# Products of 512, 256 and 384 columns over token parts side by side, exponentials and row steps kept away from the ends of gate sums, and spaced copies of rpb

## The chip, the cores and the metric

The kernel runs on one core of one Trainium2 chip. The metric is the time of one execution on the device, in microseconds; several runs are taken and their median counts. Besides the timed runs there is one profiled execution, and every row of the trace in this document is from such an execution. The engines are named as in the profile: PE is the matrix engine, PEld its loading of weights, DVE the vector engine, ACT the scalar engine, POOL GpSimd, SP the engine that issues most transfers. A "product" is one matrix multiplication instruction of PE.

## The reference

One layer of a hybrid diffusion backbone, in float32, for 128 context tokens and 256 latent tokens (384 tokens in all), with 2048 channels:

```python
sh1, sc1, g1, sh2, sc2, g2 = modulation(cond, w_mod_l, b_mod_l)
h = rms_norm(x, n1) * (1 + sc1) + sh1
q, k, v, u = project_in(h, w_in_l, qg_l, kg_l)
attn = attend(q, k, v)
# token_mixing
na = attn.reshape(b, t, D_NA) @ w_na_proj
fn = fourier_mix(u) @ w_fnet_proj
g_na, g_fn = jnp.split(jax.nn.sigmoid(h @ w_gate), 2, axis=-1)
x = x + g1 * ((g_na * na + g_fn * fn) @ w_o)
h2 = rms_norm(x, n2) * (1 + sc2) + sh2
# swiglu
a, g = jnp.split(h2 @ w_gate_up, 2, axis=-1)
x = x + g2 * ((jax.nn.silu(g) * a) @ w_down)
```

The attention of the latent tokens adds a position bias, which is gathered from the small table `rpb`.

## The kernel before

**Products in three parts.** Each operand x of a large product is kept as a high part H (x rounded to the type F32R) and a low part L = x - H. `mm3` (L146) issues three products: aH·bH, aH·bL and aL·bH. The first operand of a product is held in PE as weights, the second streams through it column by column. In the gate and the feed-forward up stages the weights are blocks of 128x128 of the weight matrix (wH, wL) and the streamed operand is h, 384 token columns wide (hH and hL, separate tiles for each of the 16 channel blocks).

**Weights.** All weight matrices come through one list of units of 256 rows by 512 columns. `next_unit` (L208) splits the unit that will be needed two units later: ACT casts it to wh (L143), DVE subtracts to get wl (L144). It then lets the next transfer be issued on SP, and returns the oldest split unit. The instructions of each engine stand in the order in which the program writes them.

**Side work.** Generators that are paced by `Paced.tick` write a step of side work between units: `rows` (the modulation rows, 16 transfers of w_mod and 32 steps on DVE, L329, for each half of a row), the Fourier branch and the attention. In the gate stage `front` holds the branch and `rows`; it is ticked three times in each unit, twice in `next_unit` and once before the third of the four sums (`mid_unit`). `Paced.tick` adds the rate to what is due, returns if less than `least` is due, and else steps until less than one is due.

**Attention.** `attention_pair` (L846) works through the ticks of `PAIR` (L44); in a tick with `e0` or `e1` ACT makes exponentials with their sums (L932), DVE takes the reciprocal (L940) and ACT scales (L942).

**Gate sums.** Eight chunks of 512 gate columns (L1018), each with eight units and four sums `po[f]` in the four `mm` banks of PSUM, which the next chunk takes again. Behind the last unit each sum is copied to SBUF (`gst`, L1032; the first two by DVE while exponentials are recent, the others by ACT) and stored to `s_gate` in DRAM by four transfers issued by ACT (L1035). In the stage behind it `load_gates` (L1053) fetches them, ACT takes the sigmoid (L1084), and DVE multiplies the projections by it (L1092).

**Feed-forward.** Six parts; in each, for four blocks f of the hidden width, first the gate half (`half` = 1, ACT's SiLU, L1319), then the other (DVE multiplies, L1321). Sums come from a ring of seven banks (`acc_tile`). The first four blocks go through another path (`late_norm`), as the norm isn't ready yet. In the last part each product is split at once for w_down (L1323).

**rpb.** `expand_rpb` (L247) makes seven copies of 512 KB from DRAM to DRAM, which give the bias as a diagonal view. It is one of the generators in `behind` in the last input group (L656), stepped once in each unit.

Of the kernel before, what the change touches and what calls it, by code (L numbers as in the profile page):

```python
# [19 lines left out]
P = 128  # L20
# [12 lines left out]
CH = 512  # L33
# [68 lines left out]
def trunk_kernel(ctx: ExitStack, tc: tile.TileContext, io: dict):  # L102
# [47 lines left out]

    def warm_sqrt():

        warm = small.tile([P, 1], F32, tag="warm", bufs=1, name=nm("warm"))
        nc.scalar.activation(out=warm, in_=ones[:, 0:1], func=AF.Sqrt)
# [73 lines left out]

    hH = [None] * KT
    hL = [None] * KT  # L230

    def new_h(kt):
        hH[kt] = hpool.tile([P, TOK], F32R, tag=f"tH{kt}", name=nm(f"hH{kt}_"))
        hL[kt] = hpool.tile([P, TOK], F32R, tag=f"tL{kt}", name=nm(f"hL{kt}_"))
        return hH[kt], hL[kt]

    s_qkvu = [dram.tile([P, NT, CH], F32, tag=f"sq{i}", name=f"s_qkvu{i}") for i in range(8)]
    s_gate = [dram.tile([P, 4, TOK], F32, tag=f"sg{i}", name=f"s_gate{i}") for i in range(8)]
# [27 lines left out]
    with ExitStack() as ph:  # L266
# [170 lines left out]
        with ExitStack() as pha:  # L437
# [377 lines left out]
        qks, vs, biases = [], [], []  # L815
        soft = deque(maxlen=3)
# [29 lines left out]
        def attention_pair(hp, wk, values_before):  # L846
# [171 lines left out]
        for fc8 in range(8):  # L1018
            po = [mm_tile() for _ in range(4)]
            sts = []  # L1020
            for u in range(0, KT, 2):
                wH, wL = next_unit()
                for f in range(4):
                    s = slice(f * P, (f + 1) * P)
                    if f == 2:
                        mid_unit()
                    for kk in range(2):
                        k = u + kk
                        mm3(po[f][:, :TOK], wH[:, kk, s], wL[:, kk, s], hH[k], hL[k], k == 0, k == KT - 1)
                    if u == KT - 2:  # L1030
                        st = gst.tile([P, TOK], F32, tag="st", name=nm("gst"))
                        (nc.vector.tensor_copy if f < 2 and any(soft) else nc.scalar.copy)(st, po[f][:, :TOK])  # L1032
                        sts.append(st)
            for f, st in enumerate(sts):
                nc.scalar.dma_start(s_gate[fc8][:, f], st)  # L1035
        br_work.drain()
        front.clear()
# [230 lines left out]

    def silus(sg, bs):
# [20 lines left out]
    for part, nf in enumerate(FF_PARTS):  # L1290
# [5 lines left out]
        for c4 in range(nf // 4):  # L1296
            for half in (1, 0):
                po = [acc_tile() for _ in range(4)]
                bs = []
                for u in range(0, KT, 2):  # L1300
                    wH, wL = next_unit()
                    for f in range(4):
                        s = slice(f * P, (f + 1) * P)
                        for kk in range(2):
                            k = u + kk
                            xH, xL = wide(k) if facc is None else (hH[k], hL[k])
                            mm3(
                                po[f][:, : xH.shape[1]], wH[:, kk, s], wL[:, kk, s], xH, xL, k == 0, k == KT - 1
                            )
# [8 lines left out]
                        elif half:  # L1318
                            nc.scalar.activation(out=sg[:, f], in_=po[f][:, :TOK], func=AF.Silu)  # L1319
                        else:  # L1320
                            nc.vector.tensor_mul(sg[:, f], sg[:, f], po[f][:, :TOK])  # L1321
                            if nf == 4:
                                work.step()  # L1323
# [84 lines left out]
```

## Time and profile before

| what | value |
|---|---|
| median of 3 runs | 2050.86 us (2049.79 to 2052.56) |
| the profiled execution | 2052.19 us |
| its span (first to last instruction) | 2050.4 us |
| mean granted clock of PE | 0.998 of full |
| PE, DVE, ACT busy | 2025.8, 1248.0, 757.9 us |
| bytes moved | 390.46 MB, mean 190 GB/s |

Rows of the trace that follow have a start in us from the beginning of the span, a duration in us, the engine, the line of kernel.py, the operation, what is written from what (`out<-in`), the shape and a count; in brackets stands how long the engine was idle before it, and what ended that wait. Matmuls overlap: the distance from start to start tells the rate of PE, not the duration of one.

### The profile page before, as it was taken

What the parts mean: (1) busy time and instruction counts of PE and PEld (TensorE: products, weight loads), DVE (VectorE), ACT (ScalarE), POOL (GpSimd) and SP (SyncE); (2) the same over time, 40 slices, a digit from 0 to 9 for tenths busy, and PEclk for the clock granted to TensorE, in tenths of its full rate; (3) what the DMA queues carried; (4) which work ended last, traced back from release to release, by engine and by line L of the source; (5) the groups of instructions that cost most, each with busy time, mean ns of one, the idle gap of its engine ahead of it and who ended that gap; (6) DMA issues with size and microseconds to landing.
All of it is one profiled execution on the core that took longest, in us unless ns stands there. A gap on an engine that the chain in (4) does not pass through costs nothing.

```text
span 2050.4 us, 27528 instructions
## 1 busy us (share of the span) xinstructions
PE 2025.8 (99%) x10986; PEld 1843.8 (90%) x10986; DVE 1248.0 (61%) x1528; ACT 757.9 (37%) x1135; POOL 43.1 (2%) x92
## 2 busy tenths in 40 slices
PE   7999999999999999999999999999999999999999
PEld 4668788999999999889998999899989998999897
DVE  4746889788987777765854444545454334333456
ACT  4433232456665434334523332222222232223222
POOL 1000000000001000010000000000000000000000
PEclk9999999999999999999999999999999999999999
DMA  9996979677776776754455555455554444444453
GB/s 332 328 338 222 309 232 315 215 217 212 228 212 181 258 248 194 250 168 154 124 167 156 152 163 155 144 153 155 155 163 134 124 129 127 129 128 123 136 163 123
DMA packets 220384, 390.46 MB, mean 190 GB/s; under 512 B 28464, under 2 KB 77632, under 8 KB 220256
## 3 DMA queue, kind: packets, MB, share of 16 engines
q1 hardware_dynamic: 213088, 382.13, 59.5%
q10 hardware_dynamic: 4672, 6.31, 0.9%
q8 instruction: 86, 1.41, 0.3%
q0 software_dynamic: 2496, 0.27, 0.1%
q14 instruction: 42, 0.34, 0.1%
HBM read 371.81 MB, written 20.51 MB: 191 GB/s over the span
## 4 chain that ended last, share of the span: by engine, by line
PE 94%; DMA 3%; DVE 2%; ACT 1%; issue 0%; SPq 0%; ACTq 0%; DVEq 0%
PE mm L147 19%; PE mm L149 19%; PE mm L148 19%; PE at L147 11%; PE at L149 11%; PE at L148 11%; PE at L404 1%; DMA wm<-in_w_mod 1%; DMA wraw<-in_w_in 1%; PE at L893 1%; PE at L979 1%; PE at L958 1%; DMA wmr<-in_w_mod 1%; DVE accr L329 0%; DMA xc<-in_x_prompt 0%
## 5 line engine op out<-in xcount | busy, mean ns | idle before, releaser
L144 DVE TENSOR_TENSOR wl<-wraw,wh 128x1024 fp32r<-128x1024 f32 (+1 forms) x464 | 559.1, 1205 | 668.5 <-ACT wh L143 667.3
L143 ACT CAST wh<-wraw 128x1024 fp32r<-128x1024 f32 (+1 forms) x464 | 480.9, 1038 | 1032.0 <-PE at L148 272.9
L147 PE MATMUL mm<-hH,wh 128*128 128x384 f32 x1152 | 389.4, 338 | 2.4 <-DVE gst L1032 2.4
L149 PE MATMUL mm<-hH,wl 128*128 128x384 f32 x1152 | 385.5, 335 | 0.0
L148 PE MATMUL mm<-hL,wh 128*128 128x384 f32 x1152 | 385.2, 334 | 0.0
L329 DVE SCALAR_TENSOR_TENSOR accr<-wmr,csz,accr 128x1024 f32<-128x1024 f32 x240 | 304.8, 1278 | 5.2 <-DMA wmr<-in_w_mod 5.1
L147 PEld LDWEIGHTS mm<-hH,wh 128*128 128x128 f32 x1152 | 216.3, 188 | 8.1 <-issue 4.3
L148 PEld LDWEIGHTS mm<-hL,wh 128*128 128x128 f32 x1152 | 216.4, 188 | 0.0
L149 PEld LDWEIGHTS mm<-hH,wl 128*128 128x128 f32 x1152 | 216.2, 188 | 0.0
L147 PE MATMUL at<-hH,wh 128*128 128x384 f32 x640 | 213.9, 334 | 0.0
L149 PE MATMUL at<-hH,wl 128*128 128x384 f32 x640 | 213.9, 334 | 0.0
L148 PE MATMUL at<-hL,wh 128*128 128x384 f32 x640 | 213.8, 334 | 0.0
L147 PE MATMUL mm<-wh,hH 128*128 128x512 f32 x404 | 160.8, 398 | 1.9 <-ACT hH L548 1.2
L148 PE MATMUL mm<-wl,hH 128*128 128x512 f32 x404 | 158.1, 391 | 2.8 <-DVE wl L144 2.8
L149 PE MATMUL mm<-wh,hL 128*128 128x512 f32 x404 | 158.4, 392 | 0.7 <-DVE hL L144 0.4
L147 PE MATMUL mm<-wh,cH 128*128 128x512 f32 x352 | 137.1, 389 | 0.0
L149 PE MATMUL mm<-wh,cL 128*128 128x512 f32 x352 | 137.0, 389 | 0.0
L148 PE MATMUL mm<-wl,cH 128*128 128x512 f32 x352 | 137.0, 389 | 0.0
L147 PEld LDWEIGHTS at<-hH,wh 128*128 128x128 f32 x640 | 120.1, 188 | 1.0 <-ACT wh L143 0.8
L148 PEld LDWEIGHTS at<-hL,wh 128*128 128x128 f32 x640 | 120.1, 188 | 0.2
L149 PEld LDWEIGHTS at<-hH,wl 128*128 128x128 f32 x640 | 120.1, 188 | 0.0
L147 PEld LDWEIGHTS mm<-wh,hH 128*128 128x128 f32 x404 | 76.0, 188 | 25.6 <-issue 3.1
(283 smaller groups left out, 2633.5 us busy)
## 6 DMA issues: line engine op xcount, KB each, us to landing
wraw<-in_w_gate_up SPq DMA_DIRECT2D x176, 512.0 KB, 3.7
wmr<-in_w_mod SPq DMA_DIRECT2D x128, 512.0 KB, 4.9
wraw<-in_w_down SPq DMA_DIRECT2D x88, 512.0 KB, 3.7
wraw<-in_w_gate SPq DMA_DIRECT2D x64, 512.0 KB, 4.3
wm<-in_w_mod SPq DMA_DIRECT2D x80, 384.0 KB, 6.7
wraw<-in_w_in SPq DMA_DIRECT2D x56, 512.0 KB, 5.8
wraw<-in_w_o SPq DMA_DIRECT2D x32, 512.0 KB, 4.7
wraw<-in_w_fnet_proj SPq DMA_DIRECT2D x16, 512.0 KB, 4.9
```

The lines of the kernel that those rows point to most:

```text
L143: nc.scalar.copy(H, x)
L144: nc.vector.tensor_sub(L, x, fr(H))
L147: nc.tensor.matmul(out, aH, bH, start=start, stop=False)
L148: nc.tensor.matmul(out, aH, bL, start=False, stop=False)
L149: nc.tensor.matmul(out, aL, bH, start=False, stop=stop)
L329: nc.vector.scalar_tensor_tensor(out=acc[:, cnd], in0=wm, scalar=sc, in1=acc[:, cnd], op0=ALU.mult, op1=ALU.add)
L404: nc.tensor.matmul(pm[q : q + 32, :w], csz[:, k, :], wm[:, ty, kk + par, :], start=k < 2, stop=k >= KT - 2, tile_position=(0, q), skip_gro ...
L893: nc.tensor.matmul(po[j][:, cols], qx[rows[j], q], kx[rows[j], k], start=i == 0, stop=i == 2, tile_position=(j * HD, 0),)
L958: nc.tensor.transpose(o[:, i * P : (i + 1) * P], sc[:, j, c0 : c0 + P], ident)
L979: nc.tensor.matmul(po[j][:, CTX:TOK].rearrange("p (t q) -> p t q", t=2), w[1 + kc], x.rearrange("p (t b) q -> p t b q", t=2)[:, :, 2 * kc ...
```

## The change

Three things are changed.

First, h's high and low part lie side by side in one tile (`hx`, 768 columns). In the gate stage and in the feed-forward up stage behind the first four blocks, `mm3_wide` takes the place of `mm3`. Its first product streams hH and the first 128 columns of hL (512 columns), the second the other 256 columns of hL with the same weights, the third hH with the low weights (384 columns). The product with the first 128 columns of hL thus lands in columns 384 to 511 of the sum and has to be added to columns 0 to 127. For the gates it is stored with them and fetched separately (`load_rest`), and DVE adds it ahead of the sigmoid. In the feed-forward part `two_parts` does it: ACT copies the 128 columns, DVE adds; what follows is then done in two pieces of 256 and 128 columns.

Second, in the last unit of each gate chunk (`ending`) attention's ticks with exponentials wait, and `rows` steps only if three steps are due.

Third, `expand_rpb` runs at a rate of 0.2.

```diff
+    def mm3_wide(out, aH, aL, b, start, stop):
+        nc.tensor.matmul(out, aH, b[:, :CH], start=start, stop=False)
+        nc.tensor.matmul(out[:, CH - TOK : TOK], aH, b[:, CH:], start=False, stop=False)
+        nc.tensor.matmul(out[:, :TOK], aL, b[:, :TOK], start=False, stop=stop)
...
     def new_h(kt):
-        hH[kt] = hpool.tile([P, TOK], F32R, tag=f"tH{kt}", name=nm(f"hH{kt}_"))
-        hL[kt] = hpool.tile([P, TOK], F32R, tag=f"tL{kt}", name=nm(f"hL{kt}_"))
+        h = hpool.tile([P, 2, TOK], F32R, tag=f"t{kt}", name=nm(f"h{kt}_"))
+        hH[kt], hL[kt] = h[:, 0], h[:, 1]
+        hx[kt] = h.rearrange("p i t -> p (i t)")
         return hH[kt], hL[kt]
...
-    s_gate = [dram.tile([P, 4, TOK], F32, tag=f"sg{i}", name=f"s_gate{i}") for i in range(8)]
+    s_gate = [dram.tile([P, 4, CH], F32, tag=f"sg{i}", name=f"s_gate{i}") for i in range(8)]
...
-                    behind.append(Paced(expand_rpb()))
+                    behind.append(Paced(expand_rpb(), 0.2))
...
             for tick in PAIR.split(","):
+                while ending[0] and "e" in tick:
+                    yield
                 for w in tick.split():
                     work[w]()
...
             for u in range(0, KT, 2):
+                ending[0] = u == KT - 2
+                rows.least = 3 if ending[0] else 1
                 wH, wL = next_unit()
...
-                        mm3(po[f][:, :TOK], wH[:, kk, s], wL[:, kk, s], hH[k], hL[k], k == 0, k == KT - 1)
+                        mm3_wide(po[f], wH[:, kk, s], wL[:, kk, s], hx[k], k == 0, k == KT - 1)
                     if u == KT - 2:
-                        st = gst.tile([P, TOK], F32, tag="st", name=nm("gst"))
-                        (nc.vector.tensor_copy if f < 2 and any(soft) else nc.scalar.copy)(st, po[f][:, :TOK])
+                        st = gst.tile([P, CH], F32, tag="st", name=nm("gst"))
+                        (nc.vector.tensor_copy if f < 2 and any(soft) else nc.scalar.copy)(st, po[f])
...
+        rows.least = 1
...
-            nc.sync.dma_start(g, s_gate[i * 4 + f4])
+            nc.sync.dma_start(g, s_gate[i * 4 + f4][:, :, :TOK])
             return g
+
+        def load_rest(f4, i):
+            g = bs.tile([P, 4, CH - TOK], F32, tag="gr", name=nm("gr"))
+            nc.sync.dma_start(g, s_gate[i * 4 + f4][:, :, TOK:])
+            return g
...
+                    if u == 0:
+                        rest = load_rest(f4, i)
                     if u == 4:
+                        g = gl[i][:, :, : CH - TOK]
+                        nc.vector.tensor_add(g, g, rest)
                         nc.scalar.activation(out=gl[i], in_=gl[i], func=AF.Sigmoid)
...
+    def two_parts(o):
+        v = actp.tile([P, P], F32, tag="fold", bufs=4, name=nm("fold"))
+        nc.scalar.copy(v, o[:, TOK:])
+        nc.vector.tensor_add(v, v, o[:, :P])
+        return (slice(P, TOK), o[:, P:TOK]), (slice(0, P), v)
...
-                            xH, xL = wide(k) if facc is None else (hH[k], hL[k])
...
+                            if facc is None:
+                                mm3(po[f][:, :XW], wH[:, kk, s], wL[:, kk, s], *wide(k), k == 0, k == KT - 1)
+                            else:
+                                mm3_wide(po[f], wH[:, kk, s], wL[:, kk, s], hx[k], k == 0, k == KT - 1)
...
-                        elif half:
-                            nc.scalar.activation(out=sg[:, f], in_=po[f][:, :TOK], func=AF.Silu)
                         else:
-                            nc.vector.tensor_mul(sg[:, f], sg[:, f], po[f][:, :TOK])
-                            if nf == 4:
+                            parts = two_parts(po[f])
+                            for sl, o in parts:
+                                if half:
+                                    nc.scalar.activation(out=sg[:, f, sl], in_=o, func=AF.Silu)
+                                else:
+                                    nc.vector.tensor_mul(sg[:, f, sl], sg[:, f, sl], o)
+                            if not half and nf == 4:
                                 work.step()
```

Three pieces of the order of instructions show what moves. The first is SP's queue in the last input group: `wraw` are weight units, `wmr` weights of the modulation rows, `s_rpb` the copies of rpb. Before:

```order
L299 DMA wmr_1702<-in_w_mod 128x1024
L250 DMA s_rpb<-in_rpb 1024x1x128
L187 DMA wraw_1705<-in_w_in 128x2x512
L299 DMA wmr_1731<-in_w_mod 128x1024
L250 DMA s_rpb<-in_rpb 1024x1x128
L187 DMA wraw_1734<-in_w_in 128x2x512
L299 DMA wmr_1760<-in_w_mod 128x1024
L250 DMA s_rpb<-in_rpb 1024x1x128
L187 DMA wraw_1763<-in_w_in 128x2x512
```

In the change, the first two copies and what lies between them (lines are those of the changed file):

```order
L259 DMA s_rpb<-in_rpb 1024x1x128
L194 DMA wraw_1801<-in_w_in 128x2x512
L194 DMA wraw_1823<-in_w_in 128x2x512
L308 DMA wmr_1848<-in_w_mod 128x1024
L633 DMA s_qkvu_89<-acc_393 128x1536
L194 DMA wraw_1852<-in_w_in 128x2x512
L308 DMA wmr_1877<-in_w_mod 128x1024
L194 DMA wraw_1880<-in_w_in 128x2x512
L308 DMA wmr_1905<-in_w_mod 128x1024
L194 DMA wraw_1908<-in_w_in 128x512
L308 DMA wmr_1933<-in_w_mod 128x1024
L259 DMA s_rpb<-in_rpb 1024x1x128
```

One copy now stands behind five weight units, where one stood behind each.

The second is DVE at the end of the fourth gate chunk. `sm` is the reciprocal of the exponentials' sums, `accr` a row step, `gst` the copy of a gate sum. Before:

```order
L144 TENSOR_TENSOR wl_4600<-wraw_4347,wh_4599 128x1024
L940 RECIPROCAL sm_4603<-sm_4603 128x2
L329 SCALAR_TENSOR_TENSOR accr_4416<-wmr_4424,csz,accr_4416 128x1024
L1032 COPY gst_4620<-mm_4114 128x384
L1032 COPY gst_4628<-mm_4115 128x384
```

In the change:

```order
L144 TENSOR_TENSOR wl_4584<-wraw_4331,wh_4583 128x1024
L1046 COPY gst_4595<-mm_4095 128x512
L1046 COPY gst_4603<-mm_4096 128x512
L950 RECIPROCAL sm_4629<-sm_4629 128x2
L338 SCALAR_TENSOR_TENSOR accr_4400<-wmr_4408,csz,accr_4400 128x1024 x2
L144 TENSOR_TENSOR wl_4640<-wraw_4381,wh_4639 128x1024
```

The copies stand ahead of the reciprocal and of the row step, which has become two; behind them comes the next weight unit's low half.

The third is ACT at the same place; L932 (L942 in the changed file) are the exponentials, L942 (L952) the scaling. Before:

```order
L143 CAST wh_4599<-wraw_4347 128x1024
L932 ACTIVATE sc_4438,sm_4603<-sc_4438,mx_4597 128x384 x2
L942 ACTIVATE sc_4438<-sc_4438,sm_4603 128x384 x2
L1032 COPY gst_4636<-mm_4116 128x384
L1032 COPY gst_4644<-mm_4117 128x384
```

In the change:

```order
L143 CAST wh_4583<-wraw_4331 128x1024
L1046 COPY gst_4611<-mm_4097 128x512
L1046 COPY gst_4619<-mm_4098 128x512
L1049 DMA s_gate_94<-gst_4595 128x512
L1049 DMA s_gate_94<-gst_4603 128x512
L1049 DMA s_gate_94<-gst_4611 128x512
L1049 DMA s_gate_94<-gst_4619 128x512
L942 ACTIVATE sc_4422,sm_4629<-sc_4422,mx_4581 128x384 x2
L952 ACTIVATE sc_4422<-sc_4422,sm_4629 128x384 x2
L143 CAST wh_4639<-wraw_4381 128x1024
```

Copies and the issue of their four transfers now come ahead of the exponentials, which stand between them and the cast of the next weight unit.

More of the change, by code (lines that the diff above doesn't have):

```diff
@@ L227, in trunk_kernel @@
     rq = consts.tile([P, NT, NH], F32, tag="rq", name="rq")
+    hx = [None] * KT
     hH = [None] * KT
@@ L815, in trunk_kernel @@
         qks, vs, biases = [], [], []
+        ending = [False]
         soft = deque(maxlen=3)
@@ L1305, in trunk_kernel @@
                             k = u + kk
-                            xH, xL = wide(k) if facc is None else (hH[k], hL[k])
-                            mm3(
-                                po[f][:, : xH.shape[1]], wH[:, kk, s], wL[:, kk, s], xH, xL, k == 0, k == KT - 1
-                            )
+                            if facc is None:
+                                mm3(po[f][:, :XW], wH[:, kk, s], wL[:, kk, s], *wide(k), k == 0, k == KT - 1)
+                            else:
+                                mm3_wide(po[f], wH[:, kk, s], wL[:, kk, s], hx[k], k == 0, k == KT - 1)
                         if u < KT - 2:
```

## The prediction

> **What bounds the kernel now.** First the head of the page with the chain of waits by engine, then one long stretch of the table by stretches (its columns: us, then busy us of PE, PE's weight loads, DVE, ACT and POOL, the granted clock, DMA share, GB/s).
>
> ```profile
> span 2050.4 us, 27528 instructions
> PE 2025.8 (99%) x10986; PEld 1843.8 (90%) x10986; DVE 1248.0 (61%) x1528; ACT 757.9 (37%) x1135; POOL 43.1 (2%) x92
> PE 94%; DMA 3%; DVE 2%; ACT 1%; issue 0%; SPq 0%; ACTq 0%; DVEq 0%
> 1030.00:2004.00 974.00, 974.00 (x5178) 915.42 (x5177) 441.55 (x444) 287.47 (x323) 6.29 (x13) 1.00 0.49 145
> ```
>
> TensorE is the bound: 94% of the chain, and in the feed-forward part (1030 to 2004 us) it never idles at full clock, with DVE busy 45% and ACT 30%. So a change can win only two things: a shorter distance between products, or one of TensorE's few waits. The distance comes from starts in the timeline of PE (start, us, what):
>
> ```profile
> 1400.03 0.33 PE L147 MATMUL mm<-hH,wh 128*128 128x384 f32 x1
> ...
> 1403.67 0.33 PE L147 MATMUL mm<-hH,wh 128*128 128x384 f32 x1
> 902.86 0.39 PE L147 MATMUL mm<-wh,hH 128*128 128x512 f32 x1
> ...
> 905.58 0.39 PE L147 MATMUL at<-wh,hH 128*128 128x512 f32 x1
> 367.21 0.28 PE L147 MATMUL at<-latH,uH 128*128 128x258 f32 x1
> ...
> 367.92 0.34 PE L147 MATMUL mm<-hH,wh 128*128 128x384 f32 x1
> 544.93 0.92 PE L979 MATMUL at<-pt,v 128*128 128x256 f32 x6
> 545.69 0.34 PE L976 MATMUL at<-pt,v 128*128 128x128 f32 x2
> ```
>
> 21 products of 384 columns take 3.64 us, 173.3 ns each; 12 of 512 take 2.72 us, 226.7 ns. Two points make a line: 53.4 ns for 128 columns and a fixed 13 ns, whatever the width. The line gives 120.0 ns for 256 columns. The trace of before has such products only in short bursts: three of 258 and three of 256 take 0.71 us (118.3 each), six behind two of 128 take 0.76 us (126.7 each).
>
> **The change part by part. The products.** A trio of 3 x 384 becomes 512 + 256 + 384: as many products, weight loads and columns (1152). By the line it takes 226.7 + 120.0 + 173.3 = 520.0 ns, and before 3 x 173.3 = 520.0. The trios: gates 8 x 16 x 4 = 512, feed-forward 80 accumulators (half and f, all but the first 8) x 16 = 1280; 1792 in all. One nanosecond more or less for the 256-column product is 1.8 us. By the bursts it is worth -1.7 ns (-3.0 us) to +6.7 ns (+12 us). I take 0, as the line rests on thousands of products and the short burst lies within 2 ns of it.
>
> [...]
>
> **rpb's transfers.** Here are the transfer queue (SP), one transfer from the chain of waits in order of time, DVE and PE around 227 us.
>
> ```profile
> 190.49 0.57 SPq L250 DMA_DIRECT2D s_rpb<-in_rpb  x1
> ...
> 208.09 0.55 SPq L250 DMA_DIRECT2D s_rpb<-in_rpb  x1
> 213.61 10.42 DMA wmr<-in_w_mod
> 224.12 2.48 DVE L329 SCALAR_TENSOR_TENSOR accr<-wmr,csz,accr 128x1024 f32<-128x1024 f32 x2 [3.89 <-DMA wmr<-in_w_mod]
> 228.31 1.22 DVE L144 TENSOR_TENSOR wl<-wraw,wh 128x1024 fp32r<-128x1024 f32 x1
> 227.18 0.39 PE L147 MATMUL mm<-wh,hH 128*128 128x512 f32 x1
> 229.58 0.50 PE L148 MATMUL mm<-wl,hH 128*128 128x512 f32 x1 [2.02 <-DVE wl L144]
> wmr<-in_w_mod SPq DMA_DIRECT2D x128, 512.0 KB, 4.9
> ```
>
> Six rpb copies in 18 us share the DMA engines with weights; the row weights issued behind them need 10.4 us instead of the usual 4.9; DVE stands 3.9 us before its row step, the weight half wl queued behind it is late, and PE starts its second product 2.40 us after its first instead of 0.23. Price of the wait: 2.2 us. At one copy in five weight units the copies are some 20 us apart, so 10.4 should fall back towards 4.9: I count the whole 2.2 us (bounds 0 and 2.2). What is late next: DVE's row steps and accumulations leave the weight halves little in hand there; the closest behind this place:
>
> ```profile
> 246.01 1.22 DVE L144 TENSOR_TENSOR wl<-wraw,wh 128x1024 fp32r<-128x1024 f32 x1
> 247.85 0.39 PE L147 MATMUL at<-wh,hH 128*128 128x512 f32 x1
> ```
>
> wl is done at 247.23 and its unit starts at 247.85: one row-weight transfer held up by a single copy could cost about 1 us again.
>
> **Exponentials and row steps at the ends of gate sums.** The four sums of a chunk (mm) are rewritten by the next chunk at once, so PE waits until gst has copied them. Two of the eight ends lose time; PE, DVE and ACT at the first, PE and DVE at the second:
>
> ```profile
> 505.54 0.44 PE L147 MATMUL mm<-hH,wh 128*128 128x384 f32 x1 [1.48 <-DVE gst L1032]
> 503.75 1.27 DVE L329 SCALAR_TENSOR_TENSOR accr<-wmr,csz,accr 128x1024 f32<-128x1024 f32 x1
> 504.94 1.02 DVE L1032 COPY gst<-mm 128x384 f32<-128x384 f32 x2
> 505.52 2.01 ACTq L1035 DMA_DIRECT2D s_gate<-gst  x4
> 510.59 1.22 DVE L144 TENSOR_TENSOR wl<-wraw,wh 128x1024 fp32r<-128x1024 f32 x1
> 515.35 0.42 PE L147 MATMUL mm<-hH,wh 128*128 128x384 f32 x1
> 639.42 0.44 PE L147 MATMUL mm<-hH,wh 128*128 128x384 f32 x1 [0.94 <-DVE gst L1032]
> ```
>
> DVE copies only after the reciprocal (which waits for ACT's exponentials) and a row step. In the change the order puts both copies ahead of both, and no end keeps exponentials ahead of its copies: -1.5 and -0.9 us (bounds 0 and these). The wider copies (a third more columns than two at 1.02 us) stay inside the 3.1 us that three other sums of six products give them. The postponed step adds a wait: DVE's reciprocal stands for exponentials that ACT starts only after four issues (2.0 us), with two row steps and the next wl queued behind it. From the end of the sums it is about 0.6 us for ACT's last copy, 2.0 for the issues, 1.3 for two exponentials (L932 below), 0.5 for their readouts and the reciprocal, an estimate; two row steps (2.5) and wl (1.2) follow: 8.1 us. The unit that needs this wl starts 515.35 - 505.54 = 9.8 us after the sums. It is hidden, with 1.7 us left; each tick it slips beyond that is PE's.
>
> **Added work.** The two parts of a sum come together by ACT copying 128 columns and DVE adding them; then the activation or product goes in two pieces. Nearest rows, from the groups by shape (mean ns behind the bar):
>
> ```profile
> L873 ACT CAST kH<-at 128x128 fp32r<-128x128 f32 x8 | 2.1, 264 | 0.0
> L144 DVE TENSOR_TENSOR AL<-at,AH 128x130 fp32r<-128x130 f32 x8 | 2.3, 283 | 0.0
> L1272 ACT ACTIVATE sg<-sg,bias 128x128 f32<-128x128 f32 x4 | 1.6, 391 | 0.0
> L932 ACT ACTIVATE sc<-sc,mx 128x384 f32<-128x384 f32 x32 | 19.6, 619 | 0.7
> ```
>
> An end of four sums costs ACT at most 4 x (264 + 391) = 2.6 us more in one half, DVE at most 4 x (283 + 283) = 2.3 us more in the other, as the shortened first piece takes no longer than the whole did. PE's next three sums have other banks, the fourth starts 6.2 us after the first of the old four ends, and both engines are idle over half the time there. That hides it, except in the last part, where each sum is split for the next matrix at once:
>
> ```profile
> 2010.86 0.55 DVE L1321 TENSOR_TENSOR sg<-sg,mm 128x384 f32<-128x384 f32 x1
> 2012.47 0.55 DVE L1321 TENSOR_TENSOR sg<-sg,mm 128x384 f32<-128x384 f32 x1
> 2013.61 0.50 PE L147 MATMUL at<-wh,cH 128*128 128x512 f32 x1
> ```
>
> One round DVE-ACT-DVE takes 1.6 us (2010.86 to 2012.47), and PE starts on the second cH as soon as it is there. A round grows by about 0.3 us (an addition and a second product of 0.28 each, less what the first product gets shorter), and the second cH stands behind two of them: +0.6 us (bounds 0 and 1.5). The separate gate columns add eight transfers and eight DVE additions of 512 elements (0.7 us each, an estimate from 283 ns for 130 columns and 0.55 us for 384). gl's loads from the same buffer took this long, and the tightest unit behind the first addition is this:
>
> ```profile
> DMA to landing us min/median/max: 5.8/7.0/11.0
> 682.16 0.38 SPq L187 DMA_DIRECT2D wraw<-in_w_na_proj  x1
> 687.45 1.22 DVE L144 TENSOR_TENSOR wl<-wraw,wh 128x1024 fp32r<-128x1024 f32 x1
> 692.91 0.33 PE L147 MATMUL mm<-aH,wh 128*128 128x384 f32 x1
> ```
>
> The first rest is issued behind the transfer of 682.16, so it lands at 688.5 by the median and at 693.5 by the longest, and DVE comes to it at 687.4. wl was done 4.2 us before its unit; addition and wait take 1.8 of it, at worst 6.8 (a loss of 2.6 us). I take 0, because each rest has a third of gl's bytes. The two halves of h in one tile wait for what they waited for before, by the order; 0.
>
> Sum: 0 - 2.2 - 1.5 - 0.9 + 0.6 = -4.0 us. The profiled execution took 2052.2 us, 1.8 more than its span; it lies 1.3 above the median of the runs shown. I take the same saving off the median: 2050.9 - 4.0 = **2046.9 us**; the profiled span would be about 2046.4.
>
> **The rivals.** *Cheaper products*: the 118.3 ns of the burst hold in steady flow; a further -3.0 us, 2043.9. Against it: the 384-column products next to the burst are not shown to keep 173.3. *A wait for a wait*: rpb's copies still meet row weights, or the postponed exponentials or the first rest push a wl past its unit; one of the three gains is lost or 1 to 2.6 us come back: about 2049.5. The 0.6 us at 247.85 and the 1.7 us above speak for it, the 4.2 us before 692.91 against. *Slower*: weight loads do not get behind a 256-column product. In the burst of six, 126.7 ns each, something beside columns takes time; at +6.7 ns x 1792 = +12.0 us the time is 2046.9 + 12.0 = 2058.9. It decides from 4.5 ns on (8.1 us, which outweighs 4.0 by 4.1). Against it: that burst stands behind two 128-column products, and ours behind one of 512.
>
> **How the numbers follow.** The forecast (three waits gone, trios equal within 1.5 ns, so 2.7 us either way) has 0.62, cheaper products 0.12, a wait for a wait 0.20, slower 0.06. About 0.2% (4.1 us) is what a measurement of this kernel can tell from no change; the forecast lies on that edge, so a little less than half of it, with the cheaper products, counts as faster: 0.42. Slower is 0.06, the rest, 0.52, is no change. The range reaches from the cheaper products to a lost gain, 2043.6 to 2050.6, and leaves the slower case out.
>
> **What would show it.** Right: 21 trios of the feed-forward part at 10.9 us; no wait over 0.5 us for gst or at the place of 227 us; the first products of the last matrix 0.5 to 1 us apart. Wrong: a 256-column product above 122 ns, or products of 384 and 512 columns that grow beside it; a wait for wl behind the reciprocal; rows that wait for wmr elsewhere in the last input group.

## The result, and the profile after

The changed kernel takes **2088.34 us** (median of 4 runs, 2085.56 to 2090.15), the kernel before 2050.32 beside it: ratio 1.0182, 95% interval 1.0165 to 1.0200, a loss of 38 us. The prediction was 2046.9, range 2043.6 to 2050.6. The profiled execution of after took 2090.15 us, its span is 2088.4.

The head of the page of after, then the table by stretches of after, and one row of it of before. The borders are the starts of the first weight product of each stage: input products, gate sums, mixing (fn and na projections with sigmoid), w_o, feed-forward. Columns as in the prediction: us, then busy us of PE, weight loads, DVE, ACT and POOL, granted clock, DMA share, GB/s.

```profile
span 2088.4 us, 27833 instructions
PE 2040.7 (98%) x10986; PEld 1780.2 (85%) x10986; DVE 1273.0 (61%) x1656; ACT 781.4 (37%) x1255; POOL 43.1 (2%) x92
```

```profile
24.59:330.73 306.14, 303.04 (x1511) 228.38 (x1511) 223.42 (x279) 109.47 (x148) 7.02 (x14) 0.99 0.88 296
330.73:693.66 362.93, 347.34 (x2122) 311.93 (x2121) 279.46 (x363) 193.33 (x395) 14.08 (x29) 0.98 0.69 213
693.66:841.49 147.83, 139.35 (x777) 135.61 (x777) 109.71 (x133) 53.80 (x62) 4.37 (x9) 0.98 0.72 235
841.49:985.73 144.24, 139.87 (x622) 113.63 (x622) 91.59 (x114) 51.54 (x83) 5.35 (x11) 0.98 0.60 194
985.73:2083.57 1097.84, 1097.33 (x5840) 979.36 (x5838) 553.84 (x731) 360.06 (x536) 6.29 (x13) 1.00 0.47 142
```

```profile
333.30:676.27 342.97, 339.77 (x2123) 328.27 (x2122) 280.60 (x364) 189.04 (x395) 14.08 (x29) 1.00 0.72 222
```

Against before (stages of both in the table further down) the loss has three places: gate sums +20.0 us, mixing +13.5, w_o +6.6. The input products gain 1.9, and the feed-forward part, where five sevenths of the new products are, loses 0.5. In the gates DVE and ACT have hardly more work than before (DVE 279.5 against 280.6 us, ACT 193.3 against 189.0). So PE waits for work that comes later, not for more work; and the clock column has fallen from 1.00 to 0.98.

**Gate sums.** The longest wait on PE, and what DVE and ACT did ahead of it:

```profile
603.32 0.77 PE L154 MATMUL mm<-h,wh 128*128 128x512 f32 x1 [4.64 <-DVE gst L1046]
590.85 0.95 DVE L930 TENSOR_REDUCE mx<-sc 128x2 f32<-128x768 f32 x1 [0.56 <-ACT sc L920]
593.95 0.18 DVE L950 RECIPROCAL sm<-sm 128x4 f32<-128x4 f32 x1 [1.82 <-ACT sc L942]
...
596.84 1.23 DVE L144 TENSOR_TENSOR wl<-wraw,wh 128x1024 fp32r<-128x1024 f32 x1 [1.55 <-ACT wh L143]
...
601.35 1.22 DVE L144 TENSOR_TENSOR wl<-wraw,wh 128x1024 fp32r<-128x1024 f32 x1
602.49 1.28 DVE L1046 COPY gst<-mm 128x512 f32<-128x512 f32 x2
591.84 0.62 ACT L942 ACTIVATE sc<-sc,mx 128x384 f32<-128x384 f32 x1 [0.76 <-DVE mx L930]
594.16 1.71 ACT L952 ACTIVATE sc<-sc,sm 128x384 f32<-128x384 f32 x4 [0.25 <-DVE sm L950]
595.78 1.03 ACT L143 CAST wh<-wraw 128x1024 fp32r<-128x1024 f32 x1
```

PE waits for DVE's copy of a finished sum. DVE did not stand at the copy; it is late, by about a unit (24 products, 4.2 us). It stood 1.82 us for the exponentials and 1.55 us for a weight cast that ACT made only after exponentials and scaling. The same step in the kernel before, DVE and ACT:

```profile
495.25 0.95 DVE L920 TENSOR_REDUCE mx<-sc 128x2 f32<-128x768 f32 x1 [0.62 <-ACT sc L910]
...
497.65 1.22 DVE L144 TENSOR_TENSOR wl<-wraw,wh 128x1024 fp32r<-128x1024 f32 x1
498.78 0.17 DVE L940 RECIPROCAL sm<-sm 128x4 f32<-128x4 f32 x1
495.35 1.07 ACT L143 CAST wh<-wraw 128x1024 fp32r<-128x1024 f32 x1
496.29 0.64 ACT L932 ACTIVATE sc<-sc,mx 128x384 f32<-128x384 f32 x1
```

There the weight split (cast on ACT, wl on DVE) lies between the maxima of the scores (L920, on DVE) and the exponentials (on ACT): ACT casts while DVE takes the maxima, DVE makes wl while ACT takes the exponentials, and in this step neither stands. From the start of the maxima to the end of wl it is 498.87 - 495.25 = 3.6 us before, and 598.07 - 590.85 = 7.2 us after. Over all 16 steps this distance is 2.2 to 3.6 us before; after, it is that in seven steps, and 5.8 to 7.2 us in the other nine, all behind the first hold. The waits of DVE for the exponentials show the same (450 to 680 us; us in total, times, longest), first before and then after:

```profile
DVE sm L940 <- ACT sc L932: 4.2, 8, 0.7
```

```profile
DVE sm L950 <- ACT sc L942: 18.4, 12, 3.3
```

In ACT's queue the cast stands behind the scalings, and in the trace of after it starts at 595.78, where the four scalings end (594.16 + 1.71 = 595.87), with no idle time between.

**Why nine steps and not two.** A unit has three ticks: ahead of the weight split, behind it, and in its middle. The table of steps has 15 entries, five units exactly, so before, the scores and maxima of every pair fall ahead of a split and the exponentials behind it. A hold (the change's wait of the exponentials in a chunk's last unit) ends at the next unit's first tick, wherever it began. The first one holds the sixth of the 16 exponential steps for two ticks, and from then on scores and maxima fall in the middle of a unit and exponentials in the next tick, with no split between; nothing brings them back. (The second hold, at the twelfth step, lasts a whole unit, so that one step has a split in it.)

**Mixing.** The longest wait there, on PE, DVE and ACT of after:

```profile
718.06 0.69 PE L147 MATMUL mm<-aH,wh 128*128 128x384 f32 x1 [4.48 <-DVE gl L1116]
710.88 0.69 DVE L1107 TENSOR_TENSOR gl<-gl,gr 128x512 f32<-128x512 f32 x1 [1.45 <-DMA gr<-s_gate]
714.06 1.23 DVE L144 TENSOR_TENSOR wl<-wraw,wh 128x1024 fp32r<-128x1024 f32 x1 [2.49 <-ACT wh L143]
717.45 0.55 DVE L1116 TENSOR_TENSOR gl<-gl,mm 128x384 f32<-128x384 f32 x1
711.61 1.49 ACT L1108 ACTIVATE gl<-gl 128x1536 f32<-128x1536 f32 x1 [6.42 <-DVE gl L1107]
713.00 1.03 ACT L143 CAST wh<-wraw 128x1024 fp32r<-128x1024 f32 x1
```

ACT reaches the sigmoid and stands there 6.42 us for the new addition of the "rest", the 128 separate columns. (DVE itself stood for the transfer of this first rest, but only 1.45 us.) The cast of a later unit stands behind the sigmoid, DVE stands 2.49 us for that cast, and its products with the sums, for which PE waits, stand behind. The waits of ACT between 674 and 845 us say the same of the stage; in the kernel before no sigmoid waited:

```profile
ACT gl L1108 <- DVE gl L1107: 27.8, 7, 6.4
```

The eighth sigmoid waited too, 6.81 us, which the profile puts down to a row-weight transfer. Of all these waits at most 2.8 us are the rests' transfers: DVE stood that long for them, in two of the eight additions. The last wait reaches into the w_o stage, where PE stands for a weight cast behind the last sigmoid and the casts of the mixed columns:

```profile
839.85 1.49 ACT L1108 ACTIVATE gl<-gl 128x1536 f32<-128x1536 f32 x1 [5.63 <-DVE gl L1107]
853.47 0.50 PE L147 MATMUL mm<-wh,h 128*128 128x512 f32 x1 [3.61 <-ACT wh L143]
```

**Clock.** A window of 12 us around the end of the first of the four longest waits (568, 598, 713 and 849 us; windows at the other three have 0.72 as well), and PE behind the second:

```profile
568.00:580.00 12.00, 8.79 (x39) 7.71 (x39) 9.55 (x12) 8.02 (x16) 0.00 (x0) 0.72 0.64 158
```

```profile
604.42 0.63 PE L154 MATMUL mm<-h,wh 128*128 128x512 f32 x1
605.38 0.63 PE L154 MATMUL mm<-h,wh 128*128 128x512 f32 x1
```

A trio takes 0.96 us there (604.42 to 605.38) instead of 0.52. A mean of 0.72 over 12 us is 6.7 us at half clock; the 6.82 us from 570.53, 601.25, 717.30 and 853.84 us on have 0.50 each. Most of each spell (some 6 us) falls behind PE's return, and costs it a little under half: some 10 us of the 38, an estimate from these rows. No run takes this part by itself.

### The profile page after: what moved, and what is told of

It is laid out like the page before. It is cut to its first block, busy times and chain, and to the rows that moved or that the text cites. A ratio compares the mean times of both kernels' runs of the same rounds, so it can differ in the third digit from the quotient of the medians.

```text
span 2088.4 us, 27833 instructions
## 1 busy us (share of the span) xinstructions
PE 2040.7 (98%) x10986; PEld 1780.2 (85%) x10986; DVE 1273.0 (61%) x1656; ACT 781.4 (37%) x1255; POOL 43.1 (2%) x92
## 4 chain that ended last, share of the span: by engine, by line
PE 58%; DVE 0%; ACT 0%; issue 0%
PE at L154 7%; PE mm L154 7%; PE mm L148 6%; PE mm L147 6%; PE mm L149 6%; PE mm L156 5%; PE at L156 5%; PE mm L155 4%; PE at L155 4%; PE at L147 3%; PE at L149 3%; PE at L148 3%; PE at L1176 0%; PE at L347 0%; DVE wl L144 0%; DVE x L1386 0%
## 5 line engine op out<-in xcount | busy, mean ns | idle before, releaser
L154 PE MATMUL mm<-h,wh 128*128 128x512 f32 x1152 | 456.4, 396 | 5.7 <-DVE gst L1046 5.7
L156 PE MATMUL mm<-h,wl 128*128 128x384 f32 x1152 | 387.8, 337 | 0.0
L155 PE MATMUL mm<-h,wh 128*128 128x256 f32 x1152 | 323.8, 281 | 0.0
L156 PEld LDWEIGHTS mm<-h,wl 128*128 128x128 f32 x1152 | 216.8, 188 | 48.7
L154 PE MATMUL at<-h,wh 128*128 128x512 f32 x640 | 249.8, 390 | 0.0
L154 PEld LDWEIGHTS mm<-h,wh 128*128 128x128 f32 x1152 | 218.8, 190 | 11.3 <-issue 9.4
L155 PEld LDWEIGHTS mm<-h,wh 128*128 128x128 f32 x1152 | 217.7, 189 | 0.0
L156 PE MATMUL at<-h,wl 128*128 128x384 f32 x640 | 214.4, 335 | 0.0
L155 PE MATMUL at<-h,wh 128*128 128x256 f32 x640 | 179.2, 280 | 0.0
L147 PE MATMUL mm<-wh,h 128*128 128x512 f32 x404 | 162.0, 401 | 5.5 <-ACT wh L143 3.6
L149 PE MATMUL mm<-wh,h 128*128 128x512 f32 x404 | 159.4, 394 | 0.4 <-DVE h L144 0.4
L154 PEld LDWEIGHTS at<-h,wh 128*128 128x128 f32 x640 | 120.9, 189 | 1.0 <-ACT fold L1296 0.8
L155 PEld LDWEIGHTS at<-h,wh 128*128 128x128 f32 x640 | 120.1, 188 | 0.2
```

The costliest lines, as they stand in the source:

```text
L147: nc.tensor.matmul(out, aH, bH, start=start, stop=False)
L149: nc.tensor.matmul(out, aL, bH, start=False, stop=stop)
L154: nc.tensor.matmul(out, aH, b[:, :CH], start=start, stop=False)
L155: nc.tensor.matmul(out[:, CH - TOK : TOK], aH, b[:, CH:], start=False, stop=False)
L156: nc.tensor.matmul(out[:, :TOK], aL, b[:, :TOK], start=False, stop=stop)
```

## The experiments

None of these kernels leaves work out. Stages in us, from the same borders in each trace; the last column is the median of the runs, and behind it the ratio to the kernel before of the same series.

| kernel | input | gates | mixing | w_o | feed-forward | whole | ratio, 95% |
|---|---|---|---|---|---|---|---|
| before | 308.1 | 343.0 | 134.3 | 137.6 | 1097.4 | 2050.3 | |
| after | 306.1 | 362.9 | 147.8 | 144.2 | 1097.8 | 2088.3 | 1.0165 to 1.0200 |
| c1 before, two empty ticks | 305.6 | 370.8 | 134.3 | 137.6 | 1097.4 | 2078.9 | 1.0123 to 1.0153 |
| c2 hold of a whole unit | 306.9 | 349.0 | 144.3 | 144.4 | 1097.8 | 2072.4 | 1.0090 to 1.0121 |
| c3 no hold | 305.0 | 345.0 | 145.7 | 143.5 | 1097.8 | 2068.7 | 1.0071 to 1.0101 |
| c4 gates of 384, no rest | 306.0 | 362.9 | 134.5 | 137.7 | 1097.8 | 2069.3 | 1.0071 to 1.0105 |
| d1 c3, rest ahead | 305.4 | 346.2 | 136.6 | 137.7 | 1097.8 | 2055.0 | 1.0003 to 1.0021 |
| d2 before, rpb thinned | 305.3 | 343.7 | 134.3 | 137.6 | 1097.4 | 2049.6 | 0.9984 to 1.0001 |
| d3 d2, row steps wait | 304.6 | 344.5 | 134.3 | 137.6 | 1097.4 | 2050.4 | 0.9987 to 1.0005 |
| d4 c4, split first | 305.4 | 366.7 | 134.3 | 137.6 | 1097.8 | 2072.9 | 1.0089 to 1.0117 |
| e1 before, one empty tick | 306.1 | 370.3 | 134.3 | 137.6 | 1097.4 | 2077.9 | 1.0117 to 1.0147 |
| e2 c1, later transposes | 306.1 | 374.4 | 134.3 | 137.6 | 1097.4 | 2082.9 | 1.0138 to 1.0177 |
| e3 c4, later transposes | 305.6 | 362.0 | 134.3 | 137.6 | 1097.8 | 2068.6 | 1.0068 to 1.0098 |
| e4 d2, later transposes | 305.0 | 343.8 | 134.3 | 137.6 | 1097.4 | 2050.0 | 0.9986 to 1.0005 |
| f1 c1, split first | 309.3 | 345.8 | 134.3 | 137.6 | 1097.4 | 2054.9 | 1.0012 to 1.0032 |
| f2 before, split first | 307.4 | 372.3 | 134.3 | 137.6 | 1097.4 | 2080.0 | 1.0128 to 1.0161 |
| f3 c2's hold and d1's rest | 305.8 | 348.2 | 139.1 | 137.7 | 1097.8 | 2058.4 | 1.0023 to 1.0049 |

**c1** moves the steps without anything else of the change, in attention():

```diff
                 wk = st.enter_context(tc.tile_pool(name="awk", bufs=1))
+                yield
+                yield
```

> The kernel before with two empty ticks ahead of the attention steps and nothing else, so that all exponentials fall in a unit's first tick, ahead of its weight cast, where the changed kernel has them from the sixth of the sixteen steps on. Theory A (the shifted place in the unit is what costs in the gate stage): the gate stage goes from 343 us to 358 to 370, the mixing stage stays at 134, the whole is 2065 to 2078. Rival B (the place is harmless; what costs is the wider copies, the held step or the rest): 343 us and 2049 to 2052.

Gates 370.8 us, 27.8 more than before (a little above the range of Theory A), and the stages behind them unchanged. The shifted place alone costs what the gate stage of after lost, and more; all 16 steps are shifted here.

**c2** holds a whole unit, **c3** not at all:

```diff
                 while ending[0] and "e" in tick:
                     yield
+                    yield
+                    yield
```

> The changed kernel with the hold lengthened to three ticks, one whole unit, so that the exponentials come back to the second tick, behind the weight cast. Theory A: the gate stage falls from 363 us to 343 to 347, the whole to 2066 to 2072; what is left over 2050 is the mixing stage and what follows. Rival (the hold itself costs, or the wider copies): 2085 to 2090.

> The changed kernel without the hold on exponentials; the row steps still wait for the ends. Theory A: gate stage 343 to 346 us, the whole 2066 to 2072, with the two waits for gst of the kernel before back (1.5 and 0.9 us). Rival (wider copies or row steps that come in bursts cost in the gate stage): 355 us and more, 2078 to 2090.

c3 takes the gate stage back to 345.0 us and 19.6 us off the whole. Its two waits for gst did not come back as expected: they are 0.4 us each, and a new one of 1.77 us, for ACT's copy, stands at the end of the sixth chunk. c2 leaves the stage at 349.0, 2 us above what was expected: PE waits 1.05 us at the end of the fourth chunk and 3.17 us at another, the sixth chunk's, where DVE's copies stand behind the pair's second scores, their maxima and a wl, and half clock for 3.41 us follows. In both, the mixing stage stays close to that of after (144.3 and 145.7 against 147.8).

**c4** leaves the gates' sums as they were:

```diff
-                        mm3_wide(po[f], wH[:, kk, s], wL[:, kk, s], hx[k], k == 0, k == KT - 1)
+                        mm3(po[f][:, :TOK], wH[:, kk, s], wL[:, kk, s], hH[k], hL[k], k == 0, k == KT - 1)
...
-                    if u == 0:
-                        rest = load_rest(f4, i)
                     if u == 4:
-                        g = gl[i][:, :, : CH - TOK]
-                        nc.vector.tensor_add(g, g, rest)
                         nc.scalar.activation(out=gl[i], in_=gl[i], func=AF.Sigmoid)
```

> The changed kernel with the gates' sums of 384 columns as before: no separate columns to load and add, so the sigmoid waits for no addition. The feed-forward part keeps the wide products and the hold stays. Theory B for the mixing stage (ACT stands in the sigmoid for the addition, and the weight casts queue behind it): mixing 148 us back to 134 to 136, the stage after it 144 to 138 to 140, the whole 2068 to 2072, the gate stage still 360 to 365. If the mixing stage is late only because the attention steps end later: mixing 146 or more, 2084 to 2090.

Mixing and w_o are back at the times of before. The gates stay at 362.9, so neither the wider sums nor their copies are what they lose by. c4 takes 19.0 us off, c3 takes 19.6: together 38.6 where after lost 38.0, which is what two separate causes would give.

**d1** asks whether the eight additions and transfers cost, or their place. c3 with the rest a half chunk ahead:

```diff
+        rests = Ahead(load_rest, [(f4, i) for f4 in range(4) for i in (1, 0)], 1)
...
-                    if u == 0:
-                        rest = load_rest(f4, i)
-                    if u == 4:
+                    if u == (0 if f4 or not i else 4):
+                        _, rest = rests.take()
+                        rests.more()
                         g = gl[i][:, :, : CH - TOK]
                         nc.vector.tensor_add(g, g, rest)
+                    if u == 4:
                         nc.scalar.activation(out=gl[i], in_=gl[i], func=AF.Sigmoid)
```

> c3 (no hold) with each rest loaded a half chunk ahead, from two buffers, and added two units earlier, at the first unit of its half (the first of the eight stays where it was); the same transfers and additions. Theory B1 (the sigmoid stands on ACT for an addition that DVE reaches late, and the weight casts stand behind the sigmoid): the mixing stage falls from 145.7 us to 134.5 to 138, the stage behind it from 143.5 to 137.5 to 139, the whole from 2068.7 to 2051 to 2056. Rival B2 (the eight additions and transfers cost by themselves, DVE or the DMA engines being short there): the mixing stage stays at 143 or more, 2065 or more.

The same work, and mixing falls from 145.7 to 136.6 us, w_o from 143.5 to 137.7. Seven of the eight sigmoids start without a wait. The one wait of ACT that is left is for the one addition that was not moved:

```profile
ACT gl L1108 <- DVE gl L1106: 3.9, 1, 3.9
```

**d2** and **d3** take the two small parts alone, in the kernel before:

```diff
-                    behind.append(Paced(expand_rpb()))
+                    behind.append(Paced(expand_rpb(), 0.2))
...
             for u in range(0, KT, 2):
+                rows.least = 3 if u == KT - 2 else 1
                 wH, wL = next_unit()
```

> The kernel before with rpb's copies thinned out and nothing else. Theory R (the wait of 2.2 us at 227 us is paid in every execution): 2.0 to 2.2 us faster, ratio 0.9989 to 0.9991. Rival (that wait came in one execution by chance, as the run with two empty ticks has rpb as before and no such wait): 0 to 0.8 us faster, ratio 0.9995 to 1.0003.

> The kernel before with rpb thinned out and the row steps waiting at the ends of the gate sums; exponentials, sums and everything else as before. If the row step ahead of the copies was the price: 1.2 us less at the first of the two ends and up to 0.9 at the second, the gate stage 341 to 342.5 us against 343.0, the whole 1 to 2 us below the kernel with rpb alone. If the row steps that come in a burst behind the end cost as much as they saved: the gate stage 343 to 345, no better than rpb alone.

d2 lies between theory and rival: 1.2 us, with an interval from 3.3 us faster to 0.2 slower. The traces say more. Waits of DVE for row weights between 180 and 330 us of the kernel before (in c1, which has rpb as before too, they come to 2.4 us, in f1 to 5.4):

```profile
DVE accr L329 <- DMA wmr<-in_w_mod: 5.1, 2, 3.9
```

All six traces with rpb as before have this wait, none of the eleven with thinned copies does. But it reaches PE unequally: 2.0 us in before, 2.3 in f1, 0.2 to 0.4 in e1, e2 and f2, none in c1 (idle time of PE; from start to start it is some 0.2 us more, 2.2 in before). In f1 the clock also fell to half for 3.41 us there (229.66 to 233.07); in before it was 1.00 from 30 to 2050 us. The input stage takes 305.6 to 309.3 us without and 304.6 to 306.9 with thinning; the means, 307.1 and 305.5, are 1.5 us apart. So the wait is real, but its 2.2 us were one execution's price; the whole times (d2) do not tell the gain from none. d3 is no better (gates 344.5 against 343.7): the waits for DVE's copies fall from 2.4 us in all to 0.6, as was meant, but PE waits 1.6 us for ACT's copy at the end of the sixth chunk instead.

**d4** was to test the first explanation of the gates, that exponentials cost when they stand ahead of the weight cast. c4 with the split first in next_unit():

```diff
+        split_unit()
         for p in front:
             p.tick()
-        split_unit()
```

> c4 (gates of 384 columns, hold as in the change, gate stage 362.9 us) with both of a unit's first two ticks behind its weight split, so that shifted exponentials no longer stand ahead of the weight cast. Theory A1 (what costs is that ACT casts a unit's weights behind exponentials and scalings): the gate stage falls to 343 to 352 us, the whole to 2049 to 2059. Rival A2 (what costs is the distance from the scaling to the transposes or some other step of the shifted cycle): 358 to 368 us, 2064 to 2075.

The total is that of the rival, but the place of the loss fits neither. The eight chunks of the gates in us, for comparison with the last series too (in c4 and d4 the first hold is in the fourth):

| | 1 | 2 | 3 | 4 | 5 | 6 | 7 | 8 |
|---|---|---|---|---|---|---|---|---|
| before | 36.7 | 45.2 | 42.8 | 47.6 | 44.3 | 42.4 | 47.1 | 36.9 |
| c4 | 36.7 | 45.4 | 42.8 | 47.4 | 46.2 | 53.5 | 48.9 | 42.0 |
| d4 | 36.7 | 49.3 | 45.6 | 56.9 | 45.6 | 46.0 | 47.3 | 39.3 |
| f1 | 36.7 | 46.5 | 42.1 | 45.8 | 44.2 | 45.6 | 47.2 | 37.7 |
| f2 | 36.7 | 48.1 | 44.0 | 58.4 | 46.6 | 50.9 | 50.7 | 36.9 |

c4 loses behind the first hold, d4 ahead of it. **e1 to e4** tried a second explanation, the way on PE between scaling and transposes; e1 has one empty tick, and e2 to e4 move the transposes in the table of steps:

```diff
-PAIR = "qk,b,pv,s0 m0,e0 i0,lq,s1 m1,e1 i1,,t0 lb,v,,t1,lv,"
+PAIR = "qk,b,pv,s0 m0,e0 i0,lq,s1 m1,e1 i1,,lb,t0 v,,,t1 lv,"
```

> The kernel before with one empty tick ahead of the attention steps, so that the exponentials fall in a unit's third tick, in its middle: behind the weight cast, but with only 36 of the sums' products between a scaling and its transposes on PE, where the kernel before has 48 and two empty ticks leave 36 as well. Theory A1 (the place ahead of the weight cast costs): gate stage 343 to 347 us, 2050 to 2055. Theory A2 (the shorter way on PE from scaling to transposes costs): gate stage 352 to 372 us, 2060 to 2080.

> The kernel with two empty ticks (gate stage 370.8 us, 2078.9) and the transposes one tick later in the table of steps: the exponentials stay ahead of the weight cast, but 48 products lie between a scaling and its transposes again. Theory A2: the gate stage falls to 343 to 355 us, the whole to 2051 to 2063. Theory A1: it stays at 362 to 374 us, 2070 to 2082.

> c4 (gates of 384 columns, the hold of the change, gate stage 362.9 us, 2069.3) with the same later transposes. Theory A2: gate stage 345 to 355 us, 2051 to 2062. Theory A1: 358 to 368 us, 2064 to 2075.

> The control, and the candidate for a better kernel: the kernel before with rpb thinned out (2049.6) and the later transposes. In its phase the next tick follows with no products between, so the way on PE stays at 48: both theories give 2048 to 2051, gate stage 342 to 344.5 us. A gate stage of 340 or less would say that the later tick gains by itself, 347 or more that it costs.

Both explanations fell. In e1 the exponentials stand behind the cast, and the gates take 370.3 us all the same. In e2 and e3 the transposes have their 48 products again, and the gates take 374.4 and 362.0. The wait for transposes at 568 us (3.19 us in c4) shrinks to 0.56 in e3, but a new one of 1.98 us stands at 547, where products need the transposed scores, and the wait for the copies at 597 us stays at 6.4. So the way on PE was not the cause.

What c1, e1, the shifted part of after and the *unshifted* part of d4 share: no weight split stands between maxima and exponentials. **f1** puts it there in c1's phase, **f2** takes it away in that of before, both with d4's edit:

> The kernel before with two empty ticks (gate stage 370.8 us as c1) and both of a unit's first two ticks behind its weight split. Scores and maxima then fall in the middle of a unit and the exponentials behind the next split, so a weight split stands between them in both queues again. Theory A3 (the split between maxima and exponentials fills the time in which DVE and ACT wait for each other; without it both stand still and run late): gate stage 343 to 353 us, the whole 2050 to 2061. Rival (only the phase of the kernel before is good, or moving the split costs in any phase): 360 us and more, 2067 or more.

> The kernel before, no empty ticks, with the same moved split: scores and maxima come directly ahead of the exponentials, with no split between, in all eight pairs. Theory A3: gate stage 358 to 372 us instead of 343, the whole 2065 to 2080. Rival (the order of exponentials and split matters, not what stands between): 343 to 350 us, 2050 to 2058.

f1 takes 25.0 us off c1's gate stage (345.8), f2 adds 29.3 to that of before (372.3), as the third theory has it. The same moved split gains in one phase and loses in the other, so neither the phase nor the order of split and exponentials is the cause by itself. DVE in c1 and then in f1, from the maxima to wl:

```profile
501.88 0.95 DVE L922 TENSOR_REDUCE mx<-sc 128x2 f32<-128x768 f32 x1 [0.56 <-ACT sc L912]
504.98 0.18 DVE L942 RECIPROCAL sm<-sm 128x4 f32<-128x4 f32 x1 [0.62 <-ACT sc L934]
507.87 1.23 DVE L144 TENSOR_TENSOR wl<-wraw,wh 128x1024 fp32r<-128x1024 f32 x1 [2.71 <-ACT wh L143]
```

```profile
500.10 0.95 DVE L922 TENSOR_REDUCE mx<-sc 128x2 f32<-128x768 f32 x1 [0.62 <-ACT sc L912]
502.49 1.22 DVE L144 TENSOR_TENSOR wl<-wraw,wh 128x1024 fp32r<-128x1024 f32 x1
503.63 0.17 DVE L942 RECIPROCAL sm<-sm 128x4 f32<-128x4 f32 x1
```

7.2 us without the split between, 3.6 with it, as in after and before. Over all steps it is 5.8 to 9.0 us in c1, e1 and f2, 2.2 to 5.0 in f1. DVE's wait for exponentials between 450 and 680 us, in f1 and then in f2:

```profile
DVE sm L942 <- ACT sc L934: 4.2, 8, 0.8
```

```profile
DVE sm L940 <- ACT sc L932: 17.1, 15, 1.8
```

**f3** is the whole change with both causes mended:

> The whole change with both causes mended: the hold lasts a whole unit, so the exponentials keep their phase, and each rest is loaded ahead and added two units earlier. If the two causes are all that matters: d1's 2055.0 plus the price of two held steps, 349.0 - 345.0 = 4 us, so 2057 to 2061. If they hide each other or a third cause is left: outside 2053 to 2064.

2058.4 us: nothing large is left besides the two. What remains over before (0.36%, 0.23 to 0.49) lies in the gates (348.2 against 343.0), where two steps are still held, and in mixing (139.1 against 134.3), where the first sigmoid still waits for its addition (4.92 us); no run takes these two apart further. No kernel beats the one before beyond the interval; d2 comes nearest.

## Why the prediction was wrong, point by point

- **The products: right.** "512 + 256 + 384" take 520 ns:

```profile
1400.05 0.39 PE L154 MATMUL at<-h,wh 128*128 128x512 f32 x1
1400.28 0.28 PE L155 MATMUL at<-h,wh 128*128 128x256 f32 x1
1400.40 0.34 PE L156 MATMUL at<-h,wl 128*128 128x384 f32 x1
1400.57 0.39 PE L154 MATMUL at<-h,wh 128*128 128x512 f32 x1
```

  The 256-column product takes 0.12 us, weight load and all; both rivals that priced it otherwise (cheaper, and 12 us dearer) are out. The rows give a load of 128x128 weights 0.19 us, longer than the 0.12 from this product to the next, and it is hidden all the same: from trio to trio it stays at 0.52 us.

```profile
1400.06 0.19 PEld L155 LDWEIGHTS at<-h,wh 128*128 128x128 f32 x1
2051.54 0.49 PE L147 MATMUL at<-wh,cH 128*128 128x512 f32 x1 [0.51 <-ACT cH L143]
```

  Feed-forward is 0.5 us longer, all of it at the second row, where PE waits for the split of a result: the two first products of the last matrix are 1.38 us apart, where they were 0.84. That is the term of +0.6; by it the sign "0.5 to 1 us apart" should have been some 1.4.
- **rpb: right in mechanism, a little too large.** -2.2 was the price of one execution; d2 gives -1.2, not clear of none, and the stage means -1.5.
- **Waits at the ends of gate sums: wrong.** Of -1.5 and -0.9 little came: at the first end PE waits 1.06 us for gst instead of 1.48, since the copies still stand behind the wl of 501.18:

```profile
501.18 1.23 DVE L144 TENSOR_TENSOR wl<-wraw,wh 128x1024 fp32r<-128x1024 f32 x1
502.32 1.28 DVE L1046 COPY gst<-mm 128x512 f32<-128x512 f32 x2
```

  At the second end, the seventh chunk's, no wait is left, but the steps have moved by then, and the wait of 4.64 stands at the end of the sixth, which had none before. d3 gives no gain from the row steps, and c2 against c3 a loss of 4 us (349.0 against 345.0) for the held exponentials.
- **The step that failed first: "It is hidden, with 1.7 us left".** It prices the one postponed step and then goes on as if the next steps stood where they had stood. The hold is a delay in a sequence that was in step with the units, so it moves all later steps, and what they lose by it (the split that filled the time in which ACT and DVE wait for each other) I had not seen as something of value. c1 shows its price without the hold: 27.8 us for 16 steps; c3 shows 19.6 us in the change.
- **The step that failed second: "I take 0, because each rest has a third of gl's bytes".** The transfer was priced, and DVE's share of the addition. Not priced was ACT: a sigmoid that waited for nothing now waits for an addition in DVE's queue, with the weight casts behind it. The bound of 2.6 us was for one wl; the stage lost 13.5, and w_o 6.6 behind it. c4 shows 19.0 us, d1 that it is the place and not the work. (The landing by the median is also added up wrongly: the issue of 682.16 ends at 682.54, and 7.0 more is 689.5, not 688.5. The wl would still have been in time, so this is not what failed.)
- **Not in the sum: the clock**, some 10 us behind four long waits, by the estimate above. The rival "a wait for a wait" had the right kind of cause with a price of 1 to 2.6 us for a single occurrence; both waits came in a series.

## What to carry to other kernels

Where steps are paced against a cycle and the table divides it evenly, a delay is no local edit: write down, for each queue, what stands between an operation and the one that answers it on another engine, before and after, for all later rounds. Work that lies between two halves of a handshake is what hides it; of a new wait, ask not only whether its input is early enough but what stands in the queue behind the waiting instruction. And a long wait on TensorE can cost more than its length, where the clock falls with it, as with the four long waits of after (0.96 us for a trio behind the second, instead of 0.52).

## What the runs showed of the hardware

With its waits, PE's clock fell to half: for 3.41 us in d1 and f1, for 6.8 with each of the four waits of after above, for some 10.2 in c1, from 609.0 us on, where PE stood for 8.5 of the 13.3 us of these two windows:

```profile
606.00:609.00 3.00, 0.71 (x5) 0.39 (x3) 2.56 (x5) 1.18 (x3) 0.00 (x0) 1.00 0.47 124
609.00:619.30 10.30, 4.09 (x13) 4.02 (x14) 6.91 (x10) 6.21 (x13) 0.00 (x0) 0.50 0.71 203
```

It also fell with short waits. In d1 PE waited only 1.86 us for a sum's copy, behind six transposes; in f1 2.33 us for a weight half, behind ordinary products. The wait of d1, and the window at half clock of each:

```profile
591.78 0.50 PE L154 MATMUL mm<-h,wh 128*128 128x512 f32 x1 [1.86 <-ACT gst L1044]
592.34:595.75 3.41, 3.41 (x12) 3.05 (x11) 1.45 (x4) 2.65 (x5) 0.00 (x0) 0.50 0.96 260
229.66:233.07 3.41, 3.35 (x8) 2.70 (x9) 3.41 (x4) 0.00 (x0) 0.00 (x0) 0.50 0.58 169
```

A longer wait in c4 left it at full speed, in its window and in the 5 us behind (1.00 in both):

```profile
571.28 0.33 PE L968 MATMUL at<-ident,sc 128*128 128x128 f32 x1 [3.19 <-ACT sc L952]
567.00:572.00 5.00, 1.64 (x10) 1.13 (x9) 2.96 (x5) 3.42 (x9) 0.00 (x0) 1.00 0.60 202
```

In after PE waited 3.18 us for scalings at the same place (its transposes start at 571.33), and there the clock fell, from 570.53 us on. So the length of a wait alone does not decide here: the clock fell with waits of 1.86, 2.33 and 3.18 us and stayed with one of 3.19. What else decides, no run shows.
